# Delta-rule blocks in a fixed order: the decay a head ahead beside the values, the first convolution term on VectorE, the tanh later, keys and queries split in pairs of tiles

## The chip, the cores and the metric

One core of a Trainium2 chip runs the program. The metric is the device time of one launch in microseconds (us). TensorE is called PE in the profile, VectorE DVE, ScalarE ACT, GpSimd POOL, and SyncE, which here only issues DMAs, SP. A difference under 0.2% is about what a measurement of this kernel can't tell from no change.

## The reference, cut to what matters

One decoder layer over 2048 tokens of 1024 channels: normalise, project to 9224 columns, run two token mixers beside each other, gate and project back. The change lies in the preparation of the first mixer, a gated delta rule with 4 heads of 128 channels, worked in chunks:

```python
qkv = jax.nn.silu(causal_depthwise_conv(dn_qkv, conv_w[layer]))      # 4 taps, per channel
dq = l2_normalize(to_heads(dq)) * (HEAD_DIM ** -0.5); dk = l2_normalize(to_heads(dk))
beta = jax.nn.sigmoid(dn_b); g = -jnp.exp(dn_a_log) * jax.nn.softplus(dn_a + dn_dt_bias)
...
gc = jnp.cumsum(g, axis=-1)
decay = jnp.exp(jnp.where(causal, gc[..., :, None] - gc[..., None, :], -jnp.inf))
lower = jnp.where(strict, jnp.einsum('bhnid,bhnjd->bhnij', kb, k) * decay, 0.0)
a_intra = jnp.where(causal, jnp.einsum('bhnid,bhnjd->bhnij', q, k) * decay, 0.0)
```

The kernel works this in tiles of 128 tokens, in float32; products that need it are made of three matmuls, with each operand split in a high part and a low part (the rest).

## The kernel before, in words

The program has five stages: the projection of the second mixer with its attention beside it, then 36 *units* of 128 output columns each (`cunits`), then the inverse and the scan of the delta rule (beside the later units), then the output projections. This change touches units 3 to 14: for each head h of 4 a unit of keys, one of queries, one of values. A unit has 4 *blocks* n of 512 tokens. A block is 24 matmuls of 128x512 (L520 to L522, tile `mm`, 3 buffers), and after every 6 of them `hook` advances a *tick*. Work that is to come later is put on a list by `at(delay, fn)`, and a hook runs what is due; so `at(8, ...)` in a block places work 48 matmuls behind the block's end. I call six matmuls, one tick, a *group*.

When the matmuls of a block are done, `conv` takes the result: ACT copies it beside the last 3 columns of the block before (`xr`) and makes the first term (`acc`, L623), DVE adds the other three taps (L625), ACT takes a tanh (L627), DVE multiplies (L628, called the *gate* here). Then:

- keys, `k_block`: transposes on PE in two pairs of tiles (L659, `tp`, 2 buffers), ACT takes the squares' sums and scales (L663, L664), and `fin` makes the norms in seven small POOL operations (L672 to L678). The decay matrix E of the block is made from a DMA of cumulated decays (`gcb`, one buffer, 512 KB), a mask (L646, DVE), four DVE operations (L650) and four exponentials on ACT (L652).
- queries, `q_block`: keys and queries are split for the three matmuls (`kqh` on ACT, `kql`: keys on POOL at L695, queries on DVE at L697), two pairs of tiles are transposed and multiplied on PE (L705 to L708), DVE multiplies by E (L711, `la`), and the results go out by DMA.
- values, `v_block`: transposes (L738), scaled by ACT (L741).

Weights of the next unit come by DMA (`raw`, 3 buffers, L499), ACT makes the high part (`wh`, L78), POOL the low part (`wl`, L79). The SP queue issues all DMAs in order; one that waits holds up those behind it.

The order of instructions on each engine in these units comes from a scheduler that places what it believes ready; only the attention stage runs under `pinned`, which keeps PE, ACT, DVE and POOL in the order in which the program is written (SP stays scheduled).

## Time and profile before

| | us |
|---|---|
| median of 3 runs | 2407.89 (2403.13 to 2408.26) |
| the profiled execution's own time | 2406.66 |
| its span in the trace | 2404.7 |
| PE busy in the span | 2356.5 (98%) |
| DVE, ACT, POOL busy | 1171.0, 855.6, 827.0 |

The profiled execution is 1.2 us under the median of the runs, and its span 2.0 us under its own time. A busy PE says little here, since a matmul's record overlaps the next one's; what the blocks take is read from the distance between the starts of like instructions, in the timeline of PE.

### The profile page before, as it was taken

The numbers are of one execution on the slowest core, as the hardware profiler recorded it, in microseconds if no ns is written. First come the engines' busy times: TensorE is split into PE (matmuls) and PEld (weight loads), VectorE is DVE, ScalarE is ACT, GpSimd is POOL, SyncE is SP. The second block draws the span as 40 slices with busy tenths as digits, with TensorE's granted clock in tenths as the row PEclk, the third lists the DMA queues.
The fourth block names the chain that finished last, engine by engine and source line by source line (L and its number), as shares of the span: only waits on it lengthen the run. The fifth ranks groups of instructions, "written<-read, shape, count | busy, mean of one in ns | idle before, by whom it ended". The sixth has DMA issues, their size and how long they took to land.

```text
span 2404.7 us, 40630 instructions
## 1 busy us (share of the span) xinstructions
PE 2356.5 (98%) x13640; PEld 2140.6 (89%) x13640; DVE 1171.0 (49%) x2819; ACT 855.6 (36%) x3021; POOL 827.0 (34%) x1803
## 2 busy tenths in 40 slices
PE   8899999999999999999999999999999999999999
PEld 7899999999999999988777878888888878889988
DVE  5533334334434433344666675999444433454431
ACT  5433333344444434334665662111233313111110
POOL 6633343333333334311442451011132222433441
PEclk8999999999999999999999999999999999999999
DMA  8443344333333334233444543222566655555442
GB/s 262 162 119 107 108 122 121 101 103 108 108 95 112 112 93 123 85 95 101 123 123 115 123 107 115 70 79 75 186 198 201 177 162 161 158 176 163 145 141 75
DMA packets 378808, 307.30 MB, mean 128 GB/s; under 512 B 61352, under 2 KB 345320, under 8 KB 378216
## 3 DMA queue, kind: packets, MB, share of 16 engines
q1 hardware_dynamic: 378312, 304.64, 43.5%
q8 instruction: 108, 1.77, 0.3%
q14 instruction: 100, 0.82, 0.1%
q10 hardware_dynamic: 288, 0.07, 0.0%
HBM read 187.92 MB, written 116.69 MB: 127 GB/s over the span
## 4 chain that ended last, share of the span: by engine, by line
PE 85%; DMA 5%; POOL 3%; DVE 3%; ACT 2%; issue 2%; SPq 0%; ACTq 0%; POOLq 0%; DVEq 0%
PE mm L236 10%; PE mm L234 10%; PE mm L235 10%; PE mm L520 9%; PE mm L522 9%; PE mm L521 9%; PE mm L1012 2%; PE mm L1010 2%; PE mm L1011 2%; DMA gcb<-gcscr 2%; PE mm L993 2%; PE mm L995 2%; PE mm L994 2%; PE po L329 2%; PE tp L286 2%
## 5 line engine op out<-in xcount | busy, mean ns | idle before, releaser
L234 PE MATMUL mm<-wh,hh 128*128 128x384 f32 (+1 forms) x1536 | 556.1, 362 | 3.2 <-ACT wh L78 1.7
L236 PE MATMUL mm<-wh,hl 128*128 128x384 f32 (+1 forms) x1536 | 521.2, 339 | 1.6 <-DVE hl L135 1.5
L235 PE MATMUL mm<-wl,hh 128*128 128x384 f32 (+1 forms) x1536 | 519.8, 338 | 0.8 <-DVE wl L79 0.4
L520 PE MATMUL mm<-hh,wh 128*128 128x512 f32 x1152 | 464.4, 403 | 0.0
L522 PE MATMUL mm<-hh,wl 128*128 128x512 f32 x1152 | 455.5, 395 | 0.0
L521 PE MATMUL mm<-hl,wh 128*128 128x512 f32 x1152 | 453.1, 393 | 0.0
L234 PEld LDWEIGHTS mm<-wh,hh 128*128 128x128 f32 x1536 | 291.3, 190 | 6.8 <-ACT wh L78 2.0
L235 PEld LDWEIGHTS mm<-wl,hh 128*128 128x128 f32 x1536 | 291.9, 190 | 2.6 <-POOL wl L189 1.6
L236 PEld LDWEIGHTS mm<-wh,hl 128*128 128x128 f32 x1536 | 290.2, 189 | 3.0 <-DVE hl L135 3.0
L522 PEld LDWEIGHTS mm<-hh,wl 128*128 128x128 f32 x1152 | 217.4, 189 | 46.7
L520 PEld LDWEIGHTS mm<-hh,wh 128*128 128x128 f32 x1152 | 217.8, 189 | 42.7
L521 PEld LDWEIGHTS mm<-hl,wh 128*128 128x128 f32 x1152 | 217.9, 189 | 42.1
L259 DVE SCALAR_TENSOR_TENSOR rec<-mm,st,wqk 128x128 f32<-128x128 f32 x384 | 116.7, 345 | 266.7 <-POOL st L251 250.7
L79 POOL TENSOR_TENSOR wl<-raw,wh 128x512 fp32r<-128x512 f32 (+1 forms) x73 | 104.6, 1444 | 409.8 <-ACT wh L78 409.8
L313 ACT ACTIVATE p<-sc,ol 128x128 f32<-128x128 f32 (+1 forms) x192 | 82.1, 428 | 315.4 <-DVE ol L311 271.2
L249 POOL TENSOR_SCALAR st<-st 128x2 f32<-128x2 f32 x192 | 37.0, 193 | 399.3 <-ACT rec L245 397.9
L245 ACT ACTIVATE rec<-mm 128x128 f32<-128x128 f32 x384 | 102.8, 273 | 184.2 <-PE mm L236 171.9
L993 PE MATMUL mm<-oh,hh 128*128 128x256 f32 x512 | 143.7, 281 | 2.0 <-DVE gt L997 2.0
L995 PE MATMUL mm<-oh,hl 128*128 128x256 f32 x512 | 142.9, 279 | 0.0
L994 PE MATMUL mm<-ol,hh 128*128 128x256 f32 x512 | 142.9, 279 | 0.0
L625 DVE SCALAR_TENSOR_TENSOR acc<-xr,cw,acc 128x512 f32<-128x512 f32 x144 | 121.8, 846 | 42.3 <-ACT acc L623 38.7
L251 POOL TENSOR_TENSOR st<-st,mhalf 128x2 f32<-128x2 f32 x192 | 136.0, 708 | 16.0
(240 smaller groups left out, 4287.4 us busy)
## 6 DMA issues: line engine op xcount, KB each, us to landing
rscr<-rec SPq DMA_DIRECT2D x192, 192.0 KB, 1.9
raw<-in_w_in_dram SPq DMA_DIRECT2D x138, 256.0 KB, 3.0
qk<-rscr SPq DMA_DIRECT2D x192, 128.0 KB, 2.2
gscr<-gt SPq DMA_DIRECT2D x64, 256.0 KB, 2.4
gt<-gscr SPq DMA_DIRECT2D x64, 256.0 KB, 3.4
oscr<-ol SPq DMA_DIRECT2D x192, 65.0 KB, 2.0
oc<-oscr SPq DMA_DIRECT2D x16, 780.0 KB, 5.1
v<-rscr SPq DMA_DIRECT2D x192, 64.0 KB, 2.0
```

What stands on the lines that cost most here:

```text
L234: nc.tensor.matmul(pr[:, :w], a, wh[:, k, :w], start=(k == 0), stop=False)
L235: nc.tensor.matmul(pr[:, :w], a, wl[:, k, :w], start=False, stop=False)
L236: nc.tensor.matmul(pr[:, :w], b, wh[:, k, :w], start=False, stop=(k == KT - 1))
L251: nc.gpsimd.tensor_tensor(out=st[:, 2:4], in0=st[:, 0:2], in1=self.mhalf[:, 0:2], op=ALU.pow)
L259: nc.vector.scalar_tensor_tensor(out=qk[:, j, :], in0=pr[:, j * P:(j + 1) * P], scalar=st[:, 2 + j:3 + j], in1=s["w"][2][:, j, :], op0=ALU ...
L520: nc.tensor.matmul(pr, wh[:, k, :], a, start=(k == 0), stop=False)
L521: nc.tensor.matmul(pr, wh[:, k, :], b, start=False, stop=False)
L522: nc.tensor.matmul(pr, wl[:, k, :], a, start=False, stop=(k == KT - 1))
L625: nc.vector.scalar_tensor_tensor(out=acc, in0=xr[:, j:j + 512], scalar=w[:, j:j + 1], in1=acc, op0=ALU.mult, op1=ALU.add)
L993: nc.tensor.matmul(o, self.wbh[:, k, ms], oh[:, k, :], start=(k == b * 4), stop=False)
L994: nc.tensor.matmul(o, self.wbh[:, k, ms], ol[:, k, :], start=False, stop=False)
L995: nc.tensor.matmul(o, self.wbl[:, k, ms], oh[:, k, :], start=False, stop=(k == b * 4 + 3))
```

## The change

- Units 3 to 14 run under `pinned(False)`: PE, ACT, DVE and POOL take the written order, SP stays scheduled.
- `conv`: for keys and queries the first term is made by DVE from PSUM (new L624) in place of ACT; values keep ACT. Tanh, gate and what follows come 2 ticks later (`gate`).
- E is no longer made in the key blocks. `e_chain` makes it for the next head, one block's worth every 5 ticks from the first value block on (for the first head every 7 ticks, from the stage's start): the DMA of `gcb`, after 3 ticks the mask, now on POOL, after 4 the four DVE operations, after 5 the four exponentials. `gcb` keeps its one buffer; E is now four tiles.
- The split of keys and queries is made in two halves (`prep`), each with two ACT copies and two POOL subtractions of 128x256, into tiles with 2 buffers; DVE's share of it goes to POOL.
- The PE pairs of keys and queries come at ticks 7 and 8 in place of 8 and 9, those of values at tick 6 in place of 8.

```diff
-        nc.scalar.activation(acc, pr, AF.Identity, scale=w[:, 3:4])
+        if ct < 8:
+            nc.vector.tensor_scalar(out=acc, in0=pr, scalar1=w[:, 3:4], scalar2=None, op0=ALU.mult)
+        else:
+            nc.scalar.activation(acc, pr, AF.Identity, scale=w[:, 3:4])
...
-        nc.scalar.activation(dst, acc, AF.Tanh, scale=0.5)
-        nc.vector.scalar_tensor_tensor(out=dst, in0=dst, scalar=1.0, in1=acc, op0=ALU.add, op1=ALU.mult)
+        def gate():
+            nc.scalar.activation(dst, acc, AF.Tanh, scale=0.5)
+            nc.vector.scalar_tensor_tensor(out=dst, in0=dst, scalar=1.0, in1=acc, op0=ALU.add, op1=ALU.mult)
+            then()
+        self.at(2, gate)
...
+    def e_chain(self, h, period, n=0):
+        if h == H:
+            return
+        nc, dp = self.nc, self.dp
+        gcb = dp.tile([P, 2, 4, P], F32, name="gcb", bufs=1)
+        nc.sync.dma_start(gcb.rearrange("p a b c -> p a (b c)"),
+                          dr(self.gcscr, h * T + n * 512, [[0, P], [H * T, 2], [1, 512]]))
+        def mask():
+            nc.gpsimd.tensor_tensor(out=gcb[:, 1], in0=gcb[:, 1],
+                                    in1=self.cmask.unsqueeze(1).to_broadcast([P, 4, P]), op=ALU.add)
+        def diff():
+            E = self.E[h, n] = dp.tile([P, 4, P], F32, name="E", bufs=4)
+            for t in range(4):
+                c = h * 16 + n * 4 + t
+                nc.vector.scalar_tensor_tensor(out=E[:, t, :], in0=gcb[:, 0, t], scalar=self.ngc[:, c:c + 1],
+                                               in1=gcb[:, 1, t], op0=ALU.add, op1=ALU.add)
+        def expo():
+            E = self.E[h, n]
+            for t in range(4):
+                c = h * 16 + n * 4 + t
+                nc.scalar.activation(E[:, t, :], E[:, t, :], AF.Exp, bias=self.nlc[:, c:c + 1])
+        self.at(3, mask)
+        self.at(4, diff)
+        self.at(5, expo)
+        if n + 1 < NB:
+            self.at(period, lambda: self.e_chain(h, period, n + 1))
...
-        self.at(8, lambda: pe(0))
-        self.at(9, lambda: pe(2))
+        self.at(7, lambda: pe(0))
+        self.at(8, lambda: pe(2))
...
-        nc.scalar.activation(kqh[:, :, 0, :], kv, AF.Copy)
-        nc.gpsimd.tensor_tensor(out=kql[:, :, 0, :], in0=kv, in1=kqh[:, :, 0, :].bitcast(F32), op=ALU.subtract)
-        nc.scalar.activation(kqh[:, :, 1, :], qv, AF.Copy)
-        nc.vector.tensor_tensor(out=kql[:, :, 1, :], in0=qv, in1=kqh[:, :, 1, :].bitcast(F32), op=ALU.subtract)
+        def prep(t0):
+            kqh = dp.tile([P, 2, 2, P], F32R, name="kqh", bufs=2)
+            kql = dp.tile([P, 2, 2, P], F32R, name="kql", bufs=2)
+            kq[t0] = kqh, kql
+            for j, src in enumerate((kv, qv)):
+                nc.scalar.activation(kqh[:, :, j, :], src[:, t0:t0 + 2, :], AF.Copy)
+                nc.gpsimd.tensor_tensor(out=kql[:, :, j, :], in0=src[:, t0:t0 + 2, :], in1=kqh[:, :, j, :].bitcast(F32),
+                                        op=ALU.subtract)
...
+        self.at(4, lambda: prep(0))
+        self.at(5, lambda: prep(2))
...
-        self.at(8, pe)
+        self.at(6, pe)
```

Where it moves instructions, at three places. In these lists a name such as `st4` is cut to `st`, and `wl`/`wh` carry a buffer number that differs between the two programs.

POOL, the second head. Before, the keys' low part for the first query block (L695) stands ahead of the norms of the first key block (L672 to L678):

```order
L616 MEMSET xr 128x3
L79 TENSOR_TENSOR wl_15207<-raw,wh_15206 128x512 x2
L695 TENSOR_TENSOR kql<-kT,kqh 128x4x128
L672 TENSOR_SCALAR ss<-ss 128x4
L673 TENSOR_TENSOR ss<-ss,mhalf 128x4
L674 TENSOR_TENSOR ss<-ss,beta 128x4
L675 TENSOR_SCALAR vss<-ss 128x4
L676 TENSOR_TENSOR ss<-ss 128x4
L677 TENSOR_SCALAR nbr<-ss 128x4
L678 TENSOR_TENSOR ksn<-nbr,egc 128x4
```

And now, from the first query block on: the low parts of its first pair of tiles, the norms of the last key block (L697 to L703), a weight's low part, the low parts of its second pair:

```order
L724 TENSOR_TENSOR kql_15550<-kT_15247,kqh_15549 128x2x128
L724 TENSOR_TENSOR kql_15550<-qT_15496,kqh_15549 128x2x128
L697 TENSOR_SCALAR ss_15444<-ss_15444 128x4
L698 TENSOR_TENSOR ss_15444<-ss_15444,mhalf_70 128x4
L699 TENSOR_TENSOR ss_15444<-ss_15444,beta_13336 128x4
L700 TENSOR_SCALAR vss_13344<-ss_15444 128x4
L701 TENSOR_TENSOR ss_15444<-ss_15444 128x4
L702 TENSOR_SCALAR nbr_13342<-ss_15444 128x4
L703 TENSOR_TENSOR ksn_13343<-nbr_13342,egc_13339 128x4
L79 TENSOR_TENSOR wl1_15509<-raw_15510,wh1_15508 128x512
L724 TENSOR_TENSOR kql_15592<-kT_15247,kqh_15591 128x2x128
L724 TENSOR_TENSOR kql_15592<-qT_15496,kqh_15591 128x2x128
```

The low parts that the second pair's matmuls read have moved behind the seven norm operations of the keys and a weight's low part.

DVE, the end of the first head's values. Before, the mask and the four decay operations of the next head's second block (L646, L650) stand among the taps of its first key block, behind the last value block's gate (the first L628):

```order
L625 SCALAR_TENSOR_TENSOR acc<-xr,cw,acc 128x512 x3
L628 SCALAR_TENSOR_TENSOR qT<-qT,acc 128x512
L618 COPY xr<-xr 128x3
L646 TENSOR_TENSOR gcb<-gcb,cmask 128x512
L650 SCALAR_TENSOR_TENSOR gcb<-gcb,ngc 128x128 x3
L625 SCALAR_TENSOR_TENSOR acc<-xr,cw,acc 128x512
L650 SCALAR_TENSOR_TENSOR gcb<-gcb,ngc 128x128
L625 SCALAR_TENSOR_TENSOR acc<-xr,cw,acc 128x512 x2
L628 SCALAR_TENSOR_TENSOR kT<-kT,acc 128x512
```

Now, the third and fourth value block and the first key block:

```order
L618 COPY xr<-xr 128x3
L628 SCALAR_TENSOR_TENSOR acc<-xr,cw,acc 128x512 x3
L658 SCALAR_TENSOR_TENSOR E<-gcb,ngc 128x128 x4
L633 SCALAR_TENSOR_TENSOR qT<-qT,acc 128x512
L618 COPY xr<-xr 128x3
L628 SCALAR_TENSOR_TENSOR acc<-xr,cw,acc 128x512 x3
L658 SCALAR_TENSOR_TENSOR E<-gcb,ngc 128x128 x4
L633 SCALAR_TENSOR_TENSOR qT<-qT,acc 128x512
L624 TENSOR_SCALAR acc<-mm,cw 128x512
L628 SCALAR_TENSOR_TENSOR acc<-xr,cw,acc 128x512 x3
L633 SCALAR_TENSOR_TENSOR kT<-kT,acc 128x512
```

The decay operations (L658) now stand between a value block's convolution and its gate (L633).

ACT, the first two key blocks of the second head. Before, four exponentials (L652) stand between the first term of a key block (L623) and the next tanh (L627) there:

```order
L741 ACTIVATE st_15144<-tp,vss 128x128 x4
L623 ACTIVATE acc<-mm,cw 128x512
L694 ACTIVATE kqh<-kT 128x4x128
L652 ACTIVATE E<-gcb,nlc 128x128 x4
L627 ACTIVATE kT<-acc 128x512
L620 ACTIVATE xr<-mm 128x512
```

Now:

```order
L665 ACTIVATE E<-E,nlc 128x128 x4
L620 ACTIVATE xr<-mm 128x512
L632 ACTIVATE kT<-acc 128x512
L776 ACTIVATE st_15197<-tp,vss 128x128 x4
L665 ACTIVATE E<-E,nlc 128x128 x4
L78 ACTIVATE wh_15258<-raw 128x512
L620 ACTIVATE xr<-mm 128x512
L632 ACTIVATE kT<-acc 128x512
L688 ACTIVATE st_15257,ss<-tp 128x128
```

The copy `xr` of the first and of the second key block stands behind the exponentials of the third and fourth link of `e_chain`.

More of the change, by code (lines that the diff above doesn't have):

```diff
@@ L637, in k_block @@
             self.kT = dp.tile([P, T], F32, name="kT", bufs=1)
[L638 to L652 removed]
+        kT = self.kT[:, n * 512:(n + 1) * 512]
+        self.conv(n, 4 + h, pr, kT, lambda: self.recput(n, h, R_KT, P, kT.rearrange("p (a c) -> p a c", c=P)))
         ss = dp.tile([P, 12], F32, name="ss", bufs=2)
@@ L702, in pe @@
             for t in (t0, t0 + 1):
[L703 to L704 removed]
                 nc.tensor.transpose(pt[:, (t - t0) * P:(t - t0 + 1) * P], qT[:, t * P:(t + 1) * P], self.ident)
[L706 to L708 removed]
+            for j in (0, 1):
+                b = pk[:, j * 256:j * 256 + 256]
+                rh, rl = (a[:, j].rearrange("p a c -> p (a c)") for a in (kqh, kql))
+                nc.tensor.matmul(b, kqh[:, j, 0, :], rh, start=True, stop=False)
+                nc.tensor.matmul(b, kqh[:, j, 0, :], rl, start=False, stop=False)
+                nc.tensor.matmul(b, kql[:, j, 0, :], rh, start=False, stop=True)
             for t in (t0, t0 + 1):
```

47 lines of the change are left out of this document (17 added, 30 removed).

## The prediction, made before the changed kernel was run

> **What bounds it now.** I read the page first: the span, the engines' shares, and the chain that ended last.
>
> ```profile
> span 2404.7 us, 40630 instructions
> PE 85%; DMA 5%; POOL 3%; DVE 3%; ACT 2%; issue 2%; SPq 0%; ACTq 0%; POOLq 0%; DVEq 0%
> ```
>
> Matmuls are 85% of the chain. The change alters no matmul, so in units 3 to 14 it can win or lose only time in which PE stands still. The waits of PE in their stretch (1128 to 1466 us), and starts in PE's timeline, show how much that is now:
>
> ```profile
> PE tp L659 <- ACT st L664: 10.6, 6, 2.7
> PE sc L707 <- POOL kql L695: 2.9, 3, 2.0
> PE sc L707 <- DVE kql L697: 1.0, 3, 0.3
> ```
> ```profile
> 1139.51 0.38 PE L659 MATMUL tp<-ident,kT 128*128 128x128 f32 x2
> 1187.50 0.27 PE L705 MATMUL tp<-ident,qT 128*128 128x128 f32 x1
> 1194.98 0.27 PE L705 MATMUL tp<-ident,qT 128*128 128x128 f32 x1
> 1200.05 0.60 PE L738 MATMUL tp<-ident,qT 128*128 128x128 f32 x4
> 1206.00 0.60 PE L738 MATMUL tp<-ident,qT 128*128 128x128 f32 x4
> 1239.81 0.38 PE L659 MATMUL tp<-ident,kT 128*128 128x128 f32 x2
> 1245.76 0.38 PE L659 MATMUL tp<-ident,kT 128*128 128x128 f32 x2
> 1282.65 0.60 PE L738 MATMUL tp<-ident,qT 128*128 128x128 f32 x4
> 1365.10 0.60 PE L738 MATMUL tp<-ident,qT 128*128 128x128 f32 x4
> 1446.38 0.60 PE L738 MATMUL tp<-ident,qT 128*128 128x128 f32 x4
> 1602.14 0.39 PE L520 MATMUL mm<-hh,wh 128*128 128x512 f32 x1
> 1602.37 0.39 PE L521 MATMUL mm<-hl,wh 128*128 128x512 f32 x1
> ```
>
> Undisturbed, a matmul starts every 0.23 us (1602.14, 1602.37), a group of six takes 1.37, a value block 5.95 (1200.05 to 1206.00), a key block 5.95 (1239.81 to 1245.76), a query block 7.48 (1187.50 to 1194.98), of which 5.49 are its 24 matmuls. From a head's first values to the next's would be 4 x (5.95 + 7.48 + 5.95) = 77.5; it is 82.6, 82.5 and 81.3. So PE loses 5.1, 5.0 and 3.8 per head, and in the first (1139.51 to 1200.05, 60.5 against 8 blocks worth 53.7) 6.8: in all 20.7 us, 0.86% of the span. More can't be won.
>
> A loss is longer than its wait where the clock drops:
>
> ```profile
> 1232.38 0.69 PE L659 MATMUL tp<-ident,kT 128*128 128x128 f32 x2 [2.41 <-ACT st L664]
> 1233.30 0.63 PE L521 MATMUL mm<-hl,wh 128*128 128x512 f32 x1
> 1233.73 0.63 PE L522 MATMUL mm<-hh,wl 128*128 128x512 f32 x1
> 1230.00:1234.00 4.00, 1.62 (x5) 1.43 (x6) 1.81 (x4) 3.22 (x14) 0.98 (x2) 0.76 0.64 196
> 1312.00:1316.00 4.00, 1.69 (x9) 1.13 (x8) 1.52 (x3) 3.71 (x15) 0.49 (x2) 1.00 0.63 177
> ```
>
> After 2.4 us idle, matmuls start 0.43 apart and the granted clock (third number from the right) is 0.76; around a similar wait at 1312 it stays 1.00. A wait of 2 us or more may cost another 1 us.
>
> **The change, part by part.** The rows that give the prices (means by shape in the units' stretch, single operations, a DMA):
>
> ```profile
> 1249.99 0.38 ACT L664 ACTIVATE st<-tp,ek 128x128 f32<-128x128 f32 x1
> 1250.24 0.29 ACT L663 ACTIVATE st<-tp 128x128 f32<-128x128 f32 x1
> L627 ACT ACTIVATE kT<-acc 128x512 f32<-128x512 f32 x16 | 10.1, 632 | 21.0 <-DVE acc L625 21.0
> L623 ACT ACTIVATE acc<-mm,cw 128x512 f32<-128x512 f32 x48 | 33.4, 695 | 0.0
> L628 DVE SCALAR_TENSOR_TENSOR kT<-kT,acc 128x512 f32<-128x512 f32 x16 | 11.1, 691 | 8.5 <-ACT kT L627 8.5
> L79 POOL TENSOR_TENSOR wl<-raw,wh 128x512 fp32r<-128x512 f32 x24 | 33.2, 1383 | 36.8 <-ACT wh L78 36.8
> L1001 POOL TENSOR_TENSOR ml<-gt,mh x64: 729/748/1178, 2033.3 to 2381.1; 128x256 fp32r<-128x256 f32 x64
> 1232.93 0.23 POOL L672 TENSOR_SCALAR ss<-ss 128x4 f32<-128x4 f32 x1 [7.34 <-ACT st L663]
> 1236.45 0.40 POOL L678 TENSOR_TENSOR ksn<-nbr,egc 128x4 f32<-128x4 f32 x1
> 1202.49 2.33 DVE L625 SCALAR_TENSOR_TENSOR acc<-xr,cw,acc 128x512 f32<-128x512 f32 x3 [1.44 <-ACT acc L623]
> 1178.75 1.31 POOL L79 TENSOR_TENSOR wl<-raw,wh 128x512 fp32r<-128x512 f32 x1 [1.33 <-ACT wh L78]
> 1178.71 1.90 DVE L625 SCALAR_TENSOR_TENSOR acc<-xr,cw,acc 128x512 f32<-128x512 f32 x1
> 1158.20 1.14 DVE L650 SCALAR_TENSOR_TENSOR gcb<-gcb,ngc 128x128 f32<-128x128 f32 x4
> gcb<-gcscr SPq DMA_DIRECT2D x16, 512.0 KB, 5.2
> 1219.89 0.36 SPq L643 DMA_DIRECT2D gcb<-gcscr  x1
> 1224.72 1.42 DVE L646 TENSOR_TENSOR gcb<-gcb,cmask 128x512 f32<-128x512 f32 x1 [2.32 <-DMA gcb<-gcscr]
> 1210.33 0.36 SPq L643 DMA_DIRECT2D gcb<-gcscr  x1
> 1216.89 0.69 DVE L646 TENSOR_TENSOR gcb<-gcb,cmask 128x512 f32<-128x512 f32 x1 [2.66 <-DMA gcb<-gcscr]
> ```
>
> *First term on DVE, 32 times; tanh and gate 2 ticks later.* ACT loses 0.70 a block. DVE gains an operation without a row; the gate's 0.69 is the nearest of its size, bounds 0.4 to 1.0. Its key block then holds 0.7 + 2.3 + 0.7 = 3.7, below 5.95. PE doesn't wait for it directly: nothing, as long as the gate comes before the transposes, 7 groups or some 10 us behind the block's end. The transposes come a group sooner than now, so this cover is 1.4 thinner. Without it each block would pay its 0.7.
>
> *Halved splits.* ACT makes four copies for two, POOL four subtractions of 0.75 (the 128x256 row) for one of 1.4, DVE loses one of 0.7. On POOL they aren't free for DVE: beside a POOL subtraction of 1.31 a tap took 1.90, against 2.33 / 3 = 0.78 alone, so 1.1 more. In a query block DVE has 0.7 + 2.3 + 0.7 + 1.4 (`la`) and up to 4 x 0.55 behind POOL, 7.3 of 7.48. It keeps up, without reserve, and PE still has its 10 us: nothing, 0.5 a block if it doesn't (a rival below).
>
> *Decay beside the values.* Gone are the waits of the key transposes, where exponentials and masks held up ACT and DVE (10.6 us of the 20.7). What takes their place: `gcb` has one buffer, so a link of the chain is DMA, mask, four DVE operations, and only then the next DMA. The mask gets 1.4, as POOL's other 128x512 operation. A link is 5.2 (between 4.8, from 1219.89 to 1224.72, and 6.6, from 1210.33 to 1216.89) + 1.4 + 1.1 + 0.1 = 7.8, while value blocks come every 5.95, and now DVE's gate stands behind the link. I count from the end of the first value block's matmuls. PE ends the second block at 7.4 (its 24 matmuls and two query pairs), the third at 14.2, the fourth at 20.0, and transposes block 2, 3 and 4 at 16.9, 22.8 and 28.6 (12 matmuls into the next block but one).
> - First link: its DMA was issued two units before; its DVE operations end at 9.7, between the two `la` of the last query block.
> - Second: SP issues a `raw` ahead of the DMA, which waits for a POOL low part: ACT's high part ends at 9.8, behind the sums of the last query pair, POOL does three small operations (3/7 of 3.9) and the low part to 12.7. The DMA goes at 13.1, takes 6 beside the `raw`, is masked at 20.4, operations to 21.8, gate of the third block 22.5, due 22.8: just in time.
> - Third: issued at 22.3, landed at 27.6, masked at 29.0, operations to 30.1, gate of the fourth block 30.8 against 28.6 due. PE waits 2.1 (0.8 to 3.5 by the landing), at three heads, since the last makes none: 6.3.
>
> Behind the waiting DMA stand on SP the stores of `rec` and weights; the latter are issued a unit (24 us) ahead: nothing.
>
> *Lag in the keys.* The fourth link, issued at 30.3, ends at 37.9. Its exponentials stand ahead of the second key block's `xr` on ACT, which begins at 38.7, 4.8 behind its matmuls. It can't catch up: `xr`, taps, tanh, and eight sums and scales (0.25 apart, rows 1249.99 and 1250.24) follow each other on ACT and DVE for 0.6 + 2.3 + 0.6 + 2.2 = 5.7, and 0.5 more where a weight's high part stands between, of 5.95. A key block's first transposes need a `tp` buffer that ACT frees 4.8 after `xr` starts, and are due 10.2 after the matmuls: cover 5.4. With the weights' 0.5 twice and a tap behind POOL the lag passes it: two blocks lose 0.4 and 0.9. I take 1.0 a head (0 to 2.5): 3.0 for three.
>
> *POOL at the queries.* The second pair of the first query block now waits for seven norm operations, a weight's low part and two subtractions. From the last key pair on PE: sums at 1.3, norms 3.9 (1232.93 to 1236.85), low part 1.4, subtractions 1.5, gaps 0.3: 8.4. The matmul that needs them is due 24 matmuls and one pair later, 5.5 + 1.2 + 0.3 = 7.0. So 1.4 is lost with all else in time, 2.2 where ACT first makes the copies that stand ahead of the sums, 4.8 by my chain with the keys' lag (sums at 5.4, not 1.3), 0.2 if POOL's small operations run at their shortest. I take 4.0, near the lagging end, as the lag itself comes from rows: four heads, 16.0. The first pair waits 0 to 1.4 for the gate and its subtractions, I take 0.5: 2.0.
>
> *Start of the first head.* Its first `gcb` can go no earlier than now (the attention's tiles stand before it), and the DVE operations behind it now stand ahead of the first convolution: 1.9 at the first key transposes (0.8 to 3), then the lag as above, 1.1: 3.0.
>
> *Clock.* Four waits over 2 us at the queries, half of them paying 1: 2.0 (0 to 6). The Trainium skill (TensorE: Matmul & The Clock Gate, The HAM clock gate) puts the fall to half the clock after an idle window of about 3.4 us. This trace has it after 2.4 already, and not after each such wait. By the page alone each of the four 4.0 us waits could pay up to 1.7, an estimate of 7 in place of 2.
>
> Outside these units PE's order stays, but for the attention's last steps beside the third unit, where PE has no such wait now: nothing, 2 either way.
>
> Sum: -20.7 + 6.3 + 3.0 + 16.0 + 2.0 + 3.0 + 2.0 = +11.6. On the profiled execution's 2406.7 that is 2418.3; the median of the runs is 1.2 above it: 2419.5.
>
> **Rivals.** *The waits simply go (faster).* One mechanism: the chain of `gcb` stays ahead, so ACT isn't late in the keys and POOL's norms begin on time and run short. It decides where a link falls below 6.9, the 5 ticks between links. The queries then cost 4 x 0.8, the values and keys 3 x 0.5, the start 2, the clock 1: 7.7 for 20.7, so 2395. For it: with the mask at 0.7, as DVE has it, and a landing at 4.8 a link is 6.7. Against it: POOL's 128x512 operations take twice that.
>
> *POOL's floor alone (no change).* The lag dissolves, the queries lose 2.2 each, the values 2.1: 8.8 + 6.3 + 0.5 + 2.5 + 1.5 = 19.6 for 20.7, so 2407. For it: in the profile now ACT has waits of 20 us and more on DVE's taps, time in which it could catch up; against it, that these waits are part of the fixed order's loop.
>
> *DVE the bound in the queries (slower still).* If each halved subtraction takes 0.55 from DVE and `la` comes late, a query block loses 0.5: 16 x 0.5 more, 2427. The Trainium skill speaks for it (GPSIMD Engine Reference, Specifications): GpSimd shares its SBUF interfaces with VectorE, with contention where VectorE has two SBUF inputs, as the taps have. The trace agrees, with 1.90 for 0.78.
>
> **Chances.** Forecast 0.50, DVE the bound 0.08, POOL's floor alone 0.18, the waits go 0.24. 0.2%, some 4.8 us, is about what a measurement can tell; so slower 0.58, same 0.18, faster 0.24. The range goes from just above the faster rival, 2397, to the forecast with the queries at 4.8, the values at 3.5 and the clock at 6, 2434. The forecast's own range is 2413 to 2430.
>
> **What would show it.** Right: PE at L738 waits for POOL's L724 once in each head, some 4 us; PE at L773 waits for DVE's L633 in the fourth value block, some 2 us; POOL before its mask (L651) waits for the `gcb` DMA, and DVE before L658 for POOL; ACT's `xr` starts some 5 us behind the matmuls in the second to fourth key block; from one head's value transposes to the next's it is 85 us or more, not 82. Wrong: these stay below 80 us, L684 waits on ACT as long as L659 does now, or PE waits somewhere that I don't name, as at `la` or at the attention's end.

## The result: 2.2% slower, and the profile after

The changed kernel takes 2457.7 us (median of 4 runs, 2457.19 to 2460.58), the kernel before in the same session 2405.57 (4 runs): ratio 1.0219, 95% interval 1.0204 to 1.0234. The prediction had the direction and missed the size: 52 us more, not 12.

The page of the changed kernel: the span, the engines' busy time, and the chain that ended last:

```profile
span 2456.1 us, 40728 instructions
...
PE 2379.4 (97%) x13640; PEld 2153.9 (88%) x13640; DVE 1185.4 (48%) x2819; ACT 841.5 (34%) x3021; POOL 877.5 (36%) x1867
...
PE 80%; POOL 5%; DVE 5%; DMA 4%; ACT 4%; issue 2%; SPq 0%; POOLq 0%; ACTq 0%; DVEq 0%
```

No engine has much more to do: POOL gained 50 us of work, DVE 14, ACT lost 14. But in the chain PE fell from 85% to 80%, and POOL, DVE and ACT rose from 8% to 14% together. So the 51 us of span are time in which PE stands or runs slowly. Its waits in units 3 to 14 follow (columns: engine, tile and line that waits, whom it waits for; total us, times, longest). L684, L733 and L773 are the transposes of keys, queries and values, L737 and L738 the products of a query pair:

```profile
PE sc L738 <- POOL kql L724: 15.7, 8, 4.1
PE tp L684 <- ACT st L689: 7.5, 7, 2.0
PE tp L773 <- DVE qT L633: 7.3, 6, 2.4
PE tp L733 <- ACT st L689: 6.9, 4, 2.0
PE tp L684 <- DVE kT L633: 3.3, 2, 2.7
PE mm L522 <- POOL wl L79: 1.5, 2, 0.7
PE sc L737 <- ACT kqh L723: 0.5, 3, 0.2
```

They sum to 42.7 us where they were 14.5. The places are those that the prediction named, and three that it didn't: the queries' transposes (L733), a weight's low part (L522) and the queries' copies (L737). But 28 us of added waits don't make 51. The rest is seen after a wait, in PE's timeline at the second head's first query block:

```profile
1278.73 0.39 PE L738 MATMUL sc<-kql,kqh 128*128 128x256 f32 x1 [2.75 <-POOL kql L724]
1279.42 0.40 PE L520 MATMUL mm<-hh,wh 128*128 128x512 f32 x1
1279.66 0.40 PE L521 MATMUL mm<-hl,wh 128*128 128x512 f32 x1
...
1280.16 0.63 PE L520 MATMUL mm<-hh,wh 128*128 128x512 f32 x1
1280.59 0.63 PE L521 MATMUL mm<-hl,wh 128*128 128x512 f32 x1
...
1283.77 0.40 PE L520 MATMUL mm<-hh,wh 128*128 128x512 f32 x1
1284.01 0.39 PE L521 MATMUL mm<-hl,wh 128*128 128x512 f32 x1
```

Some 1.4 us behind the end of the wait of 2.75 us matmuls begin to start 0.43 us apart, for some 3.5 us, and then 0.24 again. In the windows view, 1240 to 1340 and 1340 to 1440 us (length, PE busy, granted clock, DMA share, GB/s), the changed kernel shows 0.95 and 0.93:

```profile
1240.00:1340.00 100.00, 90.05 (x417) 0.95 0.42 106
1340.00:1440.00 100.00, 89.51 (x406) 0.93 0.38 98
```

and the kernel before 1.00 in both:

```profile
1240.00:1340.00 100.00, 96.23 (x475) 1.00 0.46 119
1340.00:1440.00 100.00, 95.95 (x480) 1.00 0.47 116
```

Of such pairs of the units' matmuls that start 0.36 to 0.5 us apart (*slow matmuls* in the expectations) there are 78, in 13 places; before there were 7, in two. To have one time for it I take all consecutive PE instructions from 1125 to 1530 us and sum by how much each starts later than the lower quartile of like pairs (the same two lines), its wait taken off. I call it the *stretch*: 12.1 us before, 41.6 after. Waits and stretch together rise by 57.7, some 6 more than the span did, so the sum is rough; but close to half of the loss is no wait at all. Not all of the stretch is clock. The slow matmuls alone are 78 x 0.2 = 15.6 us, where they were 7 x 0.2 = 1.4: 14.2 of the 29.5. The rest lies at other pairs of instructions, among them transposes and products beside the slow matmuls, and the first instruction behind a wait; how much of it is clock isn't shown.

### The profile page after: what moved, and what is told of

Read it like the earlier page. It is cut to its first block, busy times and chain, and to the rows that moved or that the text cites. A ratio compares the mean times of both kernels' runs of the same rounds, so it can differ in the third digit from the quotient of the medians.

```text
span 2456.1 us, 40728 instructions
## 1 busy us (share of the span) xinstructions
PE 2379.4 (97%) x13640; PEld 2153.9 (88%) x13640; DVE 1185.4 (48%) x2819; ACT 841.5 (34%) x3021; POOL 877.5 (36%) x1867
## 4 chain that ended last, share of the span: by engine, by line
PE 80%; POOL 5%; DVE 5%; DMA 4%; ACT 4%; issue 2%; SPq 0%; POOLq 0%; ACTq 0%; DVEq 0%
PE mm L236 10%; PE mm L234 10%; PE mm L235 10%; PE mm L520 8%; PE mm L522 8%; PE mm L521 8%; DVE acc L628 3%; PE mm L1045 2%; PE mm L1047 2%; PE mm L1046 2%; PE mm L1028 2%; PE mm L1030 2%; PE mm L1029 2%; PE po L329 2%; PE tp L286 2%
## 5 line engine op out<-in xcount | busy, mean ns | idle before, releaser
L520 PE MATMUL mm<-hh,wh 128*128 128x512 f32 x1152 | 472.1, 410 | 0.0
L522 PE MATMUL mm<-hh,wl 128*128 128x512 f32 x1152 | 460.8, 400 | 1.5 <-POOL wl L79 1.5
L521 PE MATMUL mm<-hl,wh 128*128 128x512 f32 x1152 | 459.4, 399 | 0.0
L522 PEld LDWEIGHTS mm<-hh,wl 128*128 128x128 f32 x1152 | 221.4, 192 | 51.5 <-POOL wl L79 2.6
L521 PEld LDWEIGHTS mm<-hl,wh 128*128 128x128 f32 x1152 | 222.0, 193 | 42.4
L249 POOL TENSOR_SCALAR st<-st 128x2 f32<-128x2 f32 x192 | 36.7, 191 | 400.4 <-ACT rec L245 399.0
L628 DVE SCALAR_TENSOR_TENSOR acc<-xr,cw,acc 128x512 f32<-128x512 f32 x144 | 132.4, 920 | 30.7 <-ACT acc L626 14.7
```

The lines of the kernel that those rows point to most:

```text
L520: nc.tensor.matmul(pr, wh[:, k, :], a, start=(k == 0), stop=False)
L521: nc.tensor.matmul(pr, wh[:, k, :], b, start=False, stop=False)
L522: nc.tensor.matmul(pr, wl[:, k, :], a, start=False, stop=(k == KT - 1))
L628: nc.vector.scalar_tensor_tensor(out=acc, in0=xr[:, j:j + 512], scalar=w[:, j:j + 1], in1=acc, op0=ALU.mult, op1=ALU.add)
```

## The experiments

All were timed beside the kernel before. Medians in us; waits and stretch of PE as above, from one profiled execution each.

| kernel | median | ratio to before (95%) | waits | stretch |
|---|---|---|---|---|
| before | 2405.6 to 2408.1 | | 14.5 | 12.1 |
| changed | 2457.70 | 1.0219 (1.0204 to 1.0234) | 42.7 | 41.6 |
| e_nopin: no fixed order | 2416.40 | 1.0038 (1.0024 to 1.0052) | 21.6 | 23.8 |
| e_norms_later | 2449.51 | 1.0172 (1.0156 to 1.0188) | 41.8 | 29.1 |
| e_chain7 | 2448.74 | 1.0165 (1.0146 to 1.0183) | 39.4 | 34.6 |
| e_fill | 2452.49 | 1.0186 (1.0170 to 1.0202) | 36.9 | 27.4 |
| e_later_pairs | 2429.13 | 1.0099 (1.0084 to 1.0114) | 31.1 | 20.9 |
| e_fixed_mended | 2428.00 | 1.0093 (1.0078 to 1.0109) | 27.9 | 20.0 |
| e_tanh_later | 2438.06 | 1.0129 (1.0115 to 1.0143) | 32.9 | 25.5 |
| e_fixed_mask | 2447.25 | 1.0170 (1.0154 to 1.0185) | 36.7 | 32.1 |
| e_fixed_four | 2424.37 | 1.0073 (1.0059 to 1.0086) | 26.4 | 19.2 |
| e_fixed_five | 2419.98 | 1.0044 (1.0027 to 1.0060) | 22.9 | 21.6 |
| e_free_mask | 2404.89 | 0.9995 (0.9986 to 1.0004) | 14.4 | 12.5 |
| e_free_mask_act | 2402.91 | 0.9990 (0.9981 to 1.0000) | 13.5 | 16.6 |
| e_free_four | 2402.84 | 0.9984 (0.9976 to 0.9993) | 14.2 | 15.8 |
| e_free_five: the kernel of e_free_four again | 2401.69 | 0.9975 (0.9966 to 0.9984) | 14.8 | not taken |
| e_free_values8 | 2410.26 | 1.0013 (1.0004 to 1.0023) | 16.6 | 20.0 |
| e_free_values8_chain7 | 2409.88 | 1.0009 (1.0000 to 1.0018) | 17.0 | 14.1 |
| e_before_mask | 2419.03 | 1.0045 (1.0030 to 1.0060) | 19.6 | 18.6 |
| e_before_first | 2405.18 | 0.9990 (0.9980 to 0.9999) | 13.0 | 11.4 |

### How much is the order: e_nopin

```diff
-            pin.enter_context(pinned(False))
```

> The changed kernel with the fixed order taken off units 3 to 14 (the line that enters it is left out); everything else stays. Theory A (the loss is made of work standing in a bad written order on POOL and ACT): the scheduler is free to put the low parts ahead of the norms and the exponentials behind xr, so most of the 43 us of PE's waits and the 15 us of slow matmuls go; PE at L738 waits under 5 us in all (15.7 in the changed kernel), and the time falls by 30 us or more, to 2400 to 2425. Rival B (the chain of data itself is too long: decay chain with one buffer, halves, earlier transposes): the order makes little difference, the time stays within 12 us of 2457, and PE waits at the same lines.

41 us of the 52 went with one line, inside what theory A gave for the time. What it gave for L738 (under 5 us) was wrong. PE's waits there kept their sum, most of it in one long wait at each of three heads (4.8, 4.3 and 4.5):

```profile
PE sc L738 <- POOL kql L724: 15.6, 7, 4.8
PE tp L684 <- DVE kT L633: 4.2, 2, 3.8
PE sc L738 <- POOL xr L616: 1.3, 1, 1.3
...
```

The POOL timeline of this kernel, late in the queries of the second head, shows what it waited for, with PE's row last:

```profile
1283.55 1.26 POOL L651 TENSOR_TENSOR gcb<-gcb,cmask 128x512 f32<-128x512 f32 x1 [2.35 <-DMA gcb<-gcscr]
1284.77 1.04 POOL L755 TENSOR_TENSOR ss<-ss,mhalf 128x4 f32<-128x4 f32 x1
1285.78 0.72 POOL L724 TENSOR_TENSOR kql<-kT,kqh 128x256 fp32r<-128x256 f32 x1
...
1286.90 1.00 POOL L724 TENSOR_TENSOR kql<-qT,kqh 128x256 fp32r<-128x256 f32 x1
1287.96 0.58 PE L738 MATMUL sc<-kql,kqh 128*128 128x256 f32 x1 [4.26 <-POOL kql L724]
```

The decay mask, now on POOL, stands at a DMA that hasn't landed, and the low parts of a query pair are queued behind it.

### The mask's place: e_free_mask, e_fixed_mask, e_before_mask

```diff
-            nc.gpsimd.tensor_tensor(out=gcb[:, 1], in0=gcb[:, 1],
+            nc.vector.tensor_tensor(out=gcb[:, 1], in0=gcb[:, 1],
```

(the other way round in the kernel before).

> The changed kernel without the fixed order, and with the decay mask (L651) back on VectorE. Without the fixed order alone PE still waited 15.6 us for POOL's L724, 4.8 us of it at one place in each head, where POOL stood for 2.35 us at the mask, whose DMA had not landed, ahead of the low parts of a query pair. Theory E (the mask, waiting on POOL for its DMA, is that cost): the waits at L738 fall under 4 us in all, most of the 38 slow matmuls go, and the time falls from 2416 to 2394 to 2402, at or below the kernel before. Rival F (POOL is full there with the small operations and low parts, the mask only shows it): L738 keeps 8 us or more and the time stays above 2410. Rival G (the wait goes with the mask to VectorE, and delays taps and gates there): the waits at L738 turn into waits for DVE's L633 at the transposes, 2403 to 2412.

> The changed kernel, fixed order kept, with only the decay mask back on VectorE. Without the fixed order this alone gave 11.5 us. In the fixed order the mask is written beside values and keys, where POOL has little else, and VectorE waits for it anyway; so theory A expects the link to become 0.7 us shorter (0.7 for 1.4), PE's waits at L773 to fall by 0.7 to 2 us a head, those at L738 to stay, and the time to fall by 3 to 8 us. Rival (its place on POOL costs the same in both orders): the time falls by 10 us or more. Rival (VectorE, which now stands at the DMA, delays taps and gates): the time rises.

> The kernel before with one part of the change alone: the decay mask on POOL in place of VectorE. Theory (the mask stands on POOL at its DMA, ahead of the weights' and the keys' low parts, wherever it is): waits for POOL at L707 rise from 2.9 to 8 us or more, the time rises by 6 to 12 us. Rival (in the key blocks POOL has room, 1.4 us more in a chain of 6 and VectorE relieved of 0.7): within 4 us of the kernel before, or some us faster.

One operation of 1.3 us, 16 times, costs about the same in three settings: 11.5 us without the fixed order (2416.4 to 2404.9), 10.4 with it, and 10.9 in the kernel before (2408.1 to 2419.0). So the order is worth 41.3 us with the mask on POOL and 42.4 with it on DVE, and with both undone the loss is gone: 2404.89 is no different from the kernel before.

Without the fixed order, theory E misses its range by 3 us: L738 kept 7.2. The time is the one that rival G gave, and part of its mechanism came too, since with the mask on VectorE the values' transposes wait, which they didn't in e_nopin:

```profile
PE tp L773 <- DVE qT L633: 5.4, 4, 1.6
```

In the fixed order the rival that the place costs the same in both orders holds, and theory A was too small: the waits at L773 fell from 7.3 to 1.3 us, as far as it allowed, but L738 gave 2.1 us too and the stretch fell by 9.5. In the kernel before the cost isn't at POOL's low parts, as I expected (L707 for POOL fell from 2.9 to 1.3), but at the key transposes: DVE's decay operations now wait for POOL's mask, ScalarE's exponentials for them, and PE for what ScalarE does behind these. With the mask on POOL, and, behind the dots, the kernel before (where PE's wait was 10.6):

```profile
DVE gcb L650 <- POOL gcb L646: 29.6, 13, 4.0
PE tp L659 <- ACT st L664: 15.8, 6, 3.1
...
DVE gcb L646 <- DMA gcb<-gcscr: 26.4, 16, 3.2
```

DVE stood before too, at its own mask, for the same DMA. With 6.1 us for POOL's memset (L616) in the same place it now stands 9.3 us more, near 16 times the 0.57 by which POOL takes longer for a mask. Common to the three settings is the duration, 1.26 us on POOL where VectorE takes 0.69, in a chain for which others queue. That the duration is the cause, and not POOL's order as well, is argued and not shown: without the fixed order POOL's wait at the DMA, in front of the low parts, stands beside it.

### The loop in the fixed order: e_tanh_later

Why does the written order lose 41 us? ACT's timeline of the changed kernel, two key blocks of the third head, and DVE's:

```profile
1341.79 0.59 ACT L620 ACTIVATE xr<-mm 128x512 f32<-128x512 f32 x1
1346.61 0.63 ACT L632 ACTIVATE kT<-acc 128x512 f32<-128x512 f32 x1 [4.24 <-DVE acc L628]
...
1349.76 0.59 ACT L620 ACTIVATE xr<-mm 128x512 f32<-128x512 f32 x1
1353.53 0.63 ACT L632 ACTIVATE kT<-acc 128x512 f32<-128x512 f32 x1 [3.18 <-DVE acc L628]
1354.07 0.26 ACT L688 ACTIVATE st<-tp 128x128 f32<-128x128 f32 x1
...
1356.42 0.37 ACT L689 ACTIVATE st<-tp,ek 128x128 f32<-128x128 f32 x1
1356.69 0.59 ACT L620 ACTIVATE xr<-mm 128x512 f32<-128x512 f32 x1
```
```profile
1343.19 3.38 DVE L628 SCALAR_TENSOR_TENSOR acc<-xr,cw,acc 128x512 f32<-128x512 f32 x3
1350.38 0.75 DVE L624 TENSOR_SCALAR acc<-mm,cw 128x512 f32<-128x512 f32 x1 [2.34 <-ACT xr L620]
1351.17 2.33 DVE L628 SCALAR_TENSOR_TENSOR acc<-xr,cw,acc 128x512 f32<-128x512 f32 x3
```

ACT copies `xr`, stands 3.18 to 4.24 us at the tanh until DVE has made first term and taps, and only then makes the eight sums and scales of the block before, though their transposes have long been there. From `xr` to `xr` it is 6.93 us (1349.76 to 1356.69) and, where the taps take 3.38 in place of 2.33, 7.97 (1341.79 to 1349.76). There a weight's low part runs beside them on POOL:

```profile
1344.74 1.28 POOL L79 TENSOR_TENSOR wl<-raw,wh 128x512 fp32r<-128x512 f32 x1
```

PE needs 5.95 for a key block. So the loop, not PE, sets the pace of the key blocks. The test is to put half of the sums ahead of the tanh:

```diff
-        self.at(2, gate)
+        self.at(4, gate)
```

> The changed kernel, fixed order kept, with the tanh and the gate at tick 4 in place of 2, so that on ScalarE the sums of the first transposed pair stand ahead of the tanh and are made while VectorE works on the taps. Theory L (in the fixed order a key block is a loop of ScalarE and VectorE one behind the other: xr 0.59, first term 0.75 and taps 2.33, tanh 0.63, sums and scales 2.62, 6.93 us of 5.95 that PE takes; half of the sums beside the taps make it 5.6): PE's waits for ScalarE at L684 and L733 (7.5 and 6.9 us) fall under 2 each, from one key block to the next it is 6.0 us and not 7 to 8, the slow matmuls halve, and the time falls by 18 to 28 us, to 2430 to 2440. Rival H (the waits follow from the decay chain's lag and POOL, not from this loop): the waits for ScalarE stay above 8 us together, and the time falls by under 8 us, or rises since the gate comes 2.7 us later.

Theory L holds: PE doesn't wait for ACT at L684 and L733 at all any more (14.4 us before the edit), and the key blocks follow each other at PE's own 5.95 (here two of them, 11.90):

```profile
1243.17 0.38 PE L684 MATMUL tp<-ident,kT 128*128 128x128 f32 x2
...
1255.07 0.38 PE L684 MATMUL tp<-ident,kT 128*128 128x128 f32 x2
```

The time fell by 19.6, the lower end of the range. Part came back at once: with later gates the keys wait longer for DVE (L684 7.1, from 3.3), and at L738 PE now waits 19.7, from 15.7.

### POOL's run at the queries: e_norms_later, e_fixed_five

```diff
-                fin()
+                self.at(2, fin)
```

> The changed kernel with the seven norm operations and the store of the scaled keys two ticks later (and a third buffer for their sums), so that they stand on POOL behind the low parts of the second query pair. Theory A (POOL's order at the queries costs 15.7 us of wait at L738 and, with the clock behind it, about 7 us more): PE's waits for POOL's L724 at the first query blocks fall from 4.1, 2.75, 3.3 and 2.5 to under 1 each, the slow matmuls behind them (35 of 78) go, and the time falls by 15 to 20 us, to 2438 to 2443. Rival B (ACT is late from the keys, the norms only stand in POOL's way because they wait for ACT): the low parts wait for ACT's copies instead, the waits at L738 keep 1.5 us or more, and the time falls by under 8 us.

The time fell by 8.2 us, between the two theories and next to rival B. POOL in the changed kernel, second head, between the low parts of the first pair and of the second:

```profile
1271.26 0.23 POOL L697 TENSOR_SCALAR ss<-ss 128x4 f32<-128x4 f32 x1
1271.57 1.04 POOL L698 TENSOR_TENSOR ss<-ss,mhalf 128x4 f32<-128x4 f32 x1
...
1274.94 0.68 POOL L703 TENSOR_TENSOR ksn<-nbr,egc 128x4 f32<-128x4 f32 x1
1275.58 1.28 POOL L79 TENSOR_TENSOR wl<-raw,wh 128x512 fp32r<-128x512 f32 x1
1276.82 1.17 POOL L724 TENSOR_TENSOR kql<-kT,kqh 128x256 fp32r<-128x256 f32 x1
1277.96 0.72 POOL L724 TENSOR_TENSOR kql<-qT,kqh 128x256 fp32r<-128x256 f32 x1
```

It runs from 1271.26 to 1278.68 with hardly a gap. With the norms moved on, the wait moved too: 3.1 us in the second query block of three heads, and 18.5 at L738 in all, more than the 15.7 before. The time fell nevertheless: PE's waits have the same sum (41.8 for 42.7) in shorter pieces, the slow matmuls are 39 in place of 78, and the stretch is 12.5 us shorter. The 39 at 0.2 us are 7.8 of the 8.2: the gain is in the clock and not in the waits.

> The changed kernel, fixed order kept, with five edits: tanh at tick 4, 7 ticks between the links of the decay chain, the memset of xr and the mask on VectorE, and the keys' norms two ticks later, so that they stand on POOL behind both low parts of the first query block. With the tanh alone later, PE waited 4.4 us in each head for these low parts, behind 4.4 us of norms and 1.3 of a weight. If the norms in front of the low parts are what is left of the fixed order's loss, the wait at L738 in the first query block goes and PE's waits in all are under 12 us: 2404 to 2413. Rival (the norms then stand before the low parts of the second block, as when they alone were moved, 3.1 us a head): waits of 18 us or more, 2415 to 2425.

The rival holds. With all five edits in the fixed order, every wait for ACT and at the values is gone, and what remains is mostly POOL:

```profile
PE sc L738 <- POOL kql L724: 17.6, 8, 3.0
PE tp L684 <- DVE kT L633: 3.9, 2, 2.4
...
```

In the first two query blocks of a head POOL has eight low parts, two of weights, and the norms of a key block and a query block one behind the other. Moving them about only moved the wait. The edits' gains don't add: alone the tanh gave 19.6 us, the mask 10.4, the chain 9.0 and the norms 8.2, and these four with the memset gave 37.7.

> The changed kernel, fixed order kept, with four places mended: tanh at tick 4, 7 ticks between the links of the decay chain, the memset of xr on VectorE, and the queries' low parts back on VectorE (in halves), which takes 0.7 us per pair off POOL. If these are the loops that the fixed order runs in, PE's waits in units 3 to 14 fall from 42.7 us to under 12 and the time to 2404 to 2415, level with the kernel before. Rival (POOL's norms, low weights and the rest still meet at the queries): L738 keeps 8 us or more, and the time is 2416 to 2428. Rival (VectorE becomes late): waits for DVE at L773, L733 or L738 appear, above 2428.

This kernel put the queries' half of the low parts back on DVE, and came to 2424. That is the time of the rival that kept POOL late, but not its mechanism: the waits for POOL went to 3.0. What came is the waits for DVE of the last rival, at less than its price. In the written order DVE's low part stands behind four operations of the next block's convolution, and PE waited 4.2 us for it at three heads.

### Distance and chain: e_later_pairs, e_fixed_mended, e_chain7

```diff
-        self.at(7, lambda: pe(0))
-        self.at(8, lambda: pe(2))
+        self.at(8, lambda: pe(0))
+        self.at(9, lambda: pe(2))
...
-        self.at(6, pe)
+        self.at(8, pe)
```

> The changed kernel, fixed order kept, with the transposes back where they were: keys and queries at ticks 8 and 9, values at 8, in place of 7, 8 and 6; so each wait of PE has 1.4 us more cover (the values 2.7). Theory A' (in the fixed order the written distance is the whole cover, and it is a tick too short): waits at L773 go (7.3), those at L684 fall from 10.8 to under 5, those at L733 from 6.9 to under 2.5, those at L738 from 15.7 to under 11, half of the 78 slow matmuls go, and the time falls by 20 to 30 us, to 2428 to 2438. Rival H (the engines run in a loop with PE: later transposes make later sums, later norms and later buffers, so the distance is kept): the time falls by under 10 us.

28.6 us, in the range of theory A', and so are L773 (none left) and L733 (0.8): there the ticks taken away had been the cover. L684 kept 11.6 and L738 15.8, as rival H has it; the edit makes neither the loop nor POOL's run shorter. It is still the largest gain of a single edit within the fixed order.

> The changed kernel, fixed order kept, with three places mended together: the norms two ticks later, the transposes at the ticks of before, and the memset of xr on VectorE in place of POOL. If these three are what the fixed order has wrong: PE's waits in units 3 to 14 fall from 42.7 us to under 15, the slow matmuls from 78 to under 25, the time to 2410 to 2424. Rival H (the loop keeps the distance, each mended wait comes back at the next place, as the norms did when they alone were moved): waits of 22 us or more remain and the time stays above 2430.

2428, between the two: moving the norms and the memset as well gave 1 us more, too little to tell from none. L738 kept 12.0 us, in eight waits where e_later_pairs has 15.8 in five, and L737 rose to 5.5 from 2.9.

```diff
-            self.e_chain(h + 1, 5)
+            self.e_chain(h + 1, 7)
```

> The changed kernel with 7 ticks (9.6 us) between the links of the decay chain at every head, in place of 5, so that a link of 7.8 us ends before the next is due. Theory B (the chain of one buffer falls behind by up to 6 us and pushes the gates of the values and ACT's xr of the keys late): PE's waits at L773 (7.3 us) fall under 1.5, those at L684 and L733 for ACT (7.5 and 6.9) by half or more, those at L738 by 2 us a head in the later heads, and the time falls by 15 to 25 us. Rival A (POOL's order at the queries is the cost): only the 7.3 us at L773 and their slow matmuls go, 8 to 11 us, and the waits at L738 stay as they are. Rival D (the exponentials cost ACT the same wherever they stand in the keys): the waits only move to later key blocks, and the time stays within 5 us of 2457.

L773 lost its 7.3 us, as theories B and A had it; the waits for ACT at the keys rose to 12.0 and the time fell by 9.0. Rival A's 8 to 11 us came, and L738 kept 15.5. The chain's lag was real and sized about right at the values, but it isn't why ACT is late in the keys.

### The clock: e_fill

```diff
+            if n == 0 and t0 == 2:
+                for _ in range(10):
+                    nc.tensor.matmul(pk, kqh[:, 0, 0, :], self.hh[:, 0, 0, :], start=True, stop=True)
```

> The changed kernel with ten matmuls of 128x512 more, whose result is overwritten at once, between the transposes and the products of the second pair of each first query block, where PE waits 2.5 to 4.1 us. They take 2.3 us of that wait (9.2 us of PE in all four heads). Theory C (the slow matmuls behind such waits come from the idle time itself): of the 78 slow matmuls the 35 behind these waits go, and the time falls by 5 to 8 us although PE does more work. Rival (the clock drops for another reason, by a period or by the load before): the slow matmuls stay, and the time is within 2 us of 2457, or up to 9 us above it where the waits don't hide the added work.

Forty matmuls more, and 5.2 us less: the stretch fell from 41.6 to 27.4, and the slow matmuls from 78 to 32. The rival, that the clock falls for another reason, would have left them. So idle time in one piece costs clock.

### The rest of the change: e_free_mask_act, e_free_four, e_before_first

> As the kernel without the fixed order and with the mask on VectorE, but with the first convolution term of keys and queries back on ScalarE. My step on record cost this move at nothing, since PE has some 10 us of cover behind each block: then the time is within 3 us of that kernel, either way. Rival: VectorE, with 0.75 us less in each of 32 blocks, is the engine that is late, and the time falls by 4 to 10 us. Rival: ScalarE is late (sums, scales, exponentials and copies), 0.70 us more in each block shows at the transposes, and the time rises by 4 to 10 us.

> The kernel before with one part of the change alone: the first convolution term of keys and queries on VectorE in place of ScalarE. My step on record costs it at nothing: within 3 us of the kernel before. In the changed kernel VectorE began this operation only after ScalarE's copy of the same PSUM tile had ended (25 of 32 times 0.02 to 0.07 us after), so the two don't run beside each other, and 0.59 + 0.75 us stand where 0.59 + 0.69 stood. Rival: VectorE has 0.75 us more in each of 32 blocks and its taps and gates come late, so PE waits more than 10.6 us at L659 and the time rises by 5 to 15 us. Rival: ScalarE, 0.70 us lighter, is in time for the key transposes, and the time falls by 4 to 10 us.

The first term is worth nothing on either engine: 2.0 us less with it back on ScalarE, 1.5 less with it on VectorE in the kernel before. In the changed kernel L624 carries a wait on ScalarE in the program and starts 0.02 to 0.07 us after the copy of the same tile ends in 28 of 32 blocks (the expectation has 25), so it stands behind the copy wherever it is.

> The changed kernel without the fixed order, with the mask on VectorE, the first term on ScalarE, and the queries' low parts back on VectorE in halves. With the first three edits PE still waited 6.9 us at L738 for POOL's low parts and 3.2 at L773. Theory F' (POOL's order of small operations, norms and low parts is what is left at the queries): L738 falls under 3 us, and the time to 2396 to 2401, 0.2 to 0.4% below the kernel before, which then is what the rest of the change (decay a head ahead, halves, tanh later) is worth. Rival (VectorE is as full as POOL: the low parts wait there behind taps): L738 waits for DVE instead, 2402 to 2408, no difference from the kernel before.

The rival holds: 2402.84, and L738 waits for DVE. With fixed order, mask, first term and the queries' low parts undone, the rest of the change (decay a head ahead, halves, tanh later, earlier transposes) is worth 0.16%, and 0.25% when the same kernel was timed again (e_free_five). That is the fastest version, about what can just be told from no change, and far less than the 20.7 us lost before. In place of the old waits there are new ones, with nearly the same sum (14.2 us for 14.5):

```profile
PE tp L773 <- DVE qT L633: 7.5, 5, 1.8
PE sc L738 <- DVE kql L724: 3.3, 4, 1.4
...
PE tp L684 <- DVE kT L633: 1.6, 2, 1.4
```

> As e_free_four, with the values' transposes at tick 8 as in the kernel before, in place of 6. There PE waited 7.5 us at L773 for the values' gate on VectorE, which stands behind the mask and its DMA. Theory (the two ticks taken from the values give back what the change removes): these waits go, and the time falls by 6 to 11 us, to 2392 to 2398, 0.4 to 0.6% below the kernel before. Rival (the scheduler or the decay chain keeps the distance, and the wait comes back at the key transposes behind): within 3 us of e_free_four.

The theory fell: L773 went to 2.2, but L684 to 6.4 from 1.6 and L738 to 6.4 from 3.3, and the time rose by 7 us. The waits came back behind, as the rival has it, at more than its price. With 7 ticks in the chain as well (e_free_values8_chain7) I expected up to 4 us less, if the chain's DMA made the rest of the waits, or 3 to 8 more; it was the same, 2409.88, with the waits where they were, so the chain isn't it. Where the scheduler sets the order I can't say which of its choices costs those 7 us; that stays open. So does the kernel before in the fixed order, which wasn't tried.

## Why the prediction was wrong in size

The direction was right; two steps failed: the loop of the key blocks (*Lag in the keys*) and the clock. The waits came to 30.3 us in the prediction (6.3 + 3.0 + 16.0 + 2.0 + 3.0); measured were 42.7, 12.4 more. Beside the waits it took off 6.2 (the 20.7 of before less 14.5 of waits) and added 2.0 of clock, so 4.2 less; measured is a stretch of 29.5 more, 33.7 apart. The two differences make 46 where the miss is 38; the stretch counts some 6 too many. The larger part of the miss lies outside the waits.

- *Values, 6.3:* L773 waits 7.3 us at three heads. Right, as e_chain7 confirms, in cause and nearly in size: 5.3 at the fourth value blocks and 2.0 at the third, which were to be just in time.
- *POOL at the queries, 16.0 and 2.0:* the second pair's waits for L724 are 4.08, 2.75, 3.32 and 2.52, together 12.7, the first pair's 3.0. Right in place and order, and POOL's run of 7.4 us (predicted 8.4 from the sums on) with it. The bound of 4.8 was added up wrongly, though: sums at 5.4 in place of 1.3 make it 1.4 + 4.1 = 5.5. The range's upper end, 2434, comes out with 5.5 and not with 4.8.
- *Lag in the keys, 3.0:* this step failed. It gave the loop as 0.6 + 2.3 + 0.6 + 2.2 = 5.7 us of 5.95. The first term had been costed at nothing two paragraphs above and was left out of the loop, 0.75; sums and scales take 2.62; it is 6.93, and 8.0 beside POOL. So it isn't a lag that is caught up or not, but a pace. The waits for ACT, 7.5 at L684 and 6.9 at L733, which wasn't named, are what it costs; with half of the sums ahead of the tanh they were gone, and 19.6 us with them (e_tanh_later).
- *Cover, nothing:* the transposes come a tick or two sooner. The prediction counted the new distances in its terms for values and queries, and priced the thinner cover by itself at nothing. With the ticks of before, in the fixed order, 28.6 of the 52 us went (e_later_pairs): 7.3 of waits at L773 and 6.1 at L733, and with them 20.7 of the stretch. Part of this is the loss of the loop and of the clock again, since more cover hides a late engine.
- *Start of the first head, 3.0:* 5.3 us at the key transposes there (2.66, 1.96 and 0.66, the second of them among the waits for ACT above): too small by 2.3.
- *Clock, 2.0:* this step failed, and it is the largest miss. I took the four waits at the queries and half of 1 us for each. The changed kernel has 13 sequences of 4 to 11 slow matmuls, 15.6 us in these alone, and a part of the rest of the stretch that isn't known. Behind several waits close together the clock fell too, and a sequence can last longer than its wait. The Trainium skill (TensorE: Matmul & The Clock Gate, The HAM clock gate) has the monitor watch free-running windows of about 3.4 us; the sequence of some 3.5 us shown above agrees with that length. By the page alone I had priced the term at 7, still too little.
- *The mask:* costed as 0.7 us in a link. Its place on POOL costs 10 to 12 us in all three settings.
- *First term, nothing:* right for the time by itself, and wrong to drop from the loop.
- *Distances:* from one head's value transposes to the next's I named 85 us or more; PE's timeline has 95.4 twice:

```profile
1210.51 0.60 PE L773 MATMUL tp<-ident,qT 128*128 128x128 f32 x4
...
1305.89 0.60 PE L773 MATMUL tp<-ident,qT 128*128 128x128 f32 x4
...
1401.29 0.60 PE L773 MATMUL tp<-ident,qT 128*128 128x128 f32 x4
```

Of the rivals, "the waits simply go" didn't come even without the fixed order and with the mask on DVE: the old waits went, but new ones of 14.4 us came for the 14.5, at 2405 in place of 2395. "DVE the bound in the queries" isn't seen: PE waits for no result of DVE there. The slowing of DVE beside POOL on which it rested is (taps 3.38 for 2.33).

## What to carry to other kernels

Before an order is fixed, write down for each engine the loop from one block to the next with everything that stands in it, the waits for the other engine included, and compare it with the bottleneck's time per block: each part here was hidden by itself, and the loop was 1 us too long. Don't take away cover in the same change that fixes the order. Price waits of the bottleneck engine above their length: the kernels in the fixed order (e_fill aside) lost 1.4 to 1.9 us for each us by which PE's waits exceeded those of the kernel before. And put nothing that waits for a DMA on an engine in front of work on which the bottleneck waits, least of all on the engine that takes longer for it.

## What the runs showed of the hardware

The granted clock falls after much shorter idle times than I had thought, but not always. Over 18 of the profiled kernels, of PE's waits with no other wait in the 7 us ahead of them, at least two matmuls 0.36 to 0.5 us apart follow within 5 us in 3 of 89 cases below 1.3 us, in 7 of 42 from 1.3 to 2, in 7 of 15 from 2 to 2.5, in 13 of 17 from 2.5 to 3.2, and in all 10 above. A free-running window, as the Trainium skill's same section has it, would make the short ones a matter of luck; that no run here shows by itself.

DVE's taps and POOL's operations are longer beside each other. In the changed kernel, from 1125 to 1500 us, DVE's taps took 0.75 us (at most 0.79) in all 85 cases without a weight's low part, a `kql` or a mask on POOL beside them, and 0.81 to 1.83 in 36 of the 54 with one. The other way round, POOL's last four norm operations on 128x4 elements (L700 to L703) took 0.20 to 0.24 us in all 31 cases without a tap beside them, and 0.53 to 0.76 in 29 of the 33 with one. The power (L698) took 1.04 each time. In the row shown above the seven norms are 4.4 us long (1271.26 to 1275.62), more than three 128x512 low parts of 1.28.
